# Hybrid decoder trunk: high weight parts cast two jobs ahead into a third buffer, decays in the big pool

## Chip, cores and metric

The kernel runs on one core of a Trainium2 chip. The metric is the device time of one execution in microseconds. PE is TensorE, DVE is VectorE, ACT is ScalarE, POOL is GpSimd, and SP is the engine that issues every DMA here.

## What is computed

One decoder layer on 512 tokens of width 1024, all in float32 (cut to its flow):

```python
u = rmsnorm(x, ln1_g)
q, k, v, pool_in, z, xbc, dt_raw, gate_pre = split(u @ w_in)
y_a = dilated_attention_mixer(q, k, v, rel_bias) @ w_a      # 3 groups of 6 heads
y_b = pool_mixer(pool_in, pool_w, pool_scale) @ w_b         # causal means of 2, 4, 8, 16 steps
y_c = ssd_mixer(z, xbc, dt_raw, ...) @ w_c                  # 4 chunks of 128, 2 groups of 8 heads
gates = sigmoid(gate_pre + b_gate)
x = x + (gates[0] * y_a + gates[1] * y_b + gates[2] * y_c) @ w_o
h = causal_dwconv(rmsnorm(x, ln2_g) @ w_up)                 # 2 x 2816 columns
x = x + (silu(h[:2816]) * h[2816:]) @ w_down
return rmsnorm(x, final_g)
```

In the SSD part the decay between two tokens of a chunk is `exp(a_cs[l] - a_cs[s])` for each head.

## The kernel before

**Three products for one.** A float32 operand is written as a high part in a rounded 32-bit format (`F32R`) and a low part, which is the difference. Each matrix product is the sum of three: high by high, high by low, low by high (`mm3`, `chunk_a`). So each weight tile goes through four steps: `fetch` has SP load it from DRAM as `raw` (1 MB for a full tile), ACT casts it into the high part `wh`, DVE subtracts to get the low part `wl`, and PE uses both. `raw`, `wh` and `wl` have two buffers each.

**Jobs.** The whole kernel is a list of weight tiles with a body each, 94 jobs, run one after the other by the loop at the end of `trunk`. In the order of that list they are: pool input 0 to 3, gates of the pool branch 4 to 7, pool products 8, w_b 9 to 12, the three attention groups 13 to 27 (two jobs for v and three for q and k in each), xbc 28 to 33, gates of the attention branch 34 to 37, gates of the SSD branch and z mixed 38 to 45, w_a 46 and 47, w_c 48 to 51, w_o 52 to 59, w_up 60 to 81, w_down 82 to 93. Most have 48 matmuls of 512 columns. The w_a jobs have 36 with a smaller tile, the eight w_o jobs 24, because they are done for two blocks of 128 tokens at a time, and the last of each half of w_down 24.

**The order.** PE, ACT, DVE and POOL run in the order in which the program is written (`ORDERED`); SP's order is found by the scheduler. Between the matmuls of a job, `step()` lets waiting side work advance by one piece: attention items, SSD items, norms. So each engine's queue is a mixture of evacuations of PSUM, side work, and the preparation of weights, and an instruction that waits holds up all that is written behind it on its engine.

**Preparation.** At the start of job n its `prepare` casts the tile of job n+1 and takes its low part, then fetches n+2 and n+3 where that has not been done (a fetch waits until the buffer is free, that is until the low part of the tile two before it is taken). Up to job 33 cast and low part are made in two halves of the columns, the second half at the job's first `step()` through the list `second`. From job 34 on they are made in one piece. A few jobs are `late`: they call `prepare` from their own body (the last w_o job and the first two w_up jobs), so that norm work comes ahead of it.

**Side work at the places that the prediction speaks of.** `y_norm(gi)` norms the SSD output of one group while the w_a jobs run: PE sums squares into `pss`, DVE and ACT make the root, DVE builds the diagonal `dg`, PE spreads it over the rows (`prb`, L875), DVE scales (L878), ACT casts the result to `yth`, DVE takes `ytl` (L885); w_c needs these. `wo_jobs` adds the product to x (L930), ACT sums its squares (`junk`, L294), DVE norms it to `u` (L335), and PE transposes `u` (`uT`, L307) for w_up. `ssd_item` loads the decays of one chunk and group: two tiles `al` of 256 KB each, from their own pool `alp` of six buffers (L754 to L759), which DVE (L785), ACT (L786) and DVE (L790) turn into the masks that PE reads for `py` (L800). All other side work takes its tiles from one pool, `big`, of 52 buffers of 128 x 512 values.

Of the kernel before, what the change touches and what calls it, by code (L numbers as in the profile page):

```python
# [10 lines left out]
F32 = mybir.dt.float32  # L11
F32R = mybir.dt.float32r
# [4 lines left out]
P = 128  # L17
S = 512
# [63 lines left out]
def trunk(ctx: ExitStack, tc, out, x, rel_bias, ln1_g, w_in, b_gate, w_a, pool_w, pool_scale, w_b,  # L82
# [9 lines left out]
    cpool = ctx.enter_context(tc.tile_pool(name="const", bufs=1))  # L92
    rows = ctx.enter_context(tc.tile_pool(name="rows", bufs=1))
    wraw = ctx.enter_context(tc.tile_pool(name="wraw", bufs=2))
    wspl = ctx.enter_context(tc.tile_pool(name="wspl", bufs=2))
    upool = ctx.enter_context(tc.tile_pool(name="upool", bufs=1))
    big = ctx.enter_context(tc.tile_pool(name="big", bufs=NBIG))
    alp = ctx.enter_context(tc.tile_pool(name="alp", bufs=6))
    ypool = ctx.enter_context(tc.tile_pool(name="ypool", bufs=2))
    tiny = ctx.enter_context(tc.tile_pool(name="tiny", bufs=8))  # L100
    psum = ctx.enter_context(tc.tile_pool(name="psum", bufs=4, space=bass.MemoryType.PSUM))
# [3 lines left out]

    def T(name, dt=F32, shape=(P, S)):
        return big.tile(list(shape), dt, name=name, tag="t")

    def A(name):
        return alp.tile([P, S], F32, name=name, tag="al")  # L110

    def MM(name):
        return psum.tile([P, S], F32, name=name, tag="mm")
# [51 lines left out]
                sp.dma_start(raw[:, :, at:at + n], src[:, :, i * n:(i + 1) * n])  # L165
                at += n

    def split(job, cuts=1, later=False, eng=None, halves=False):
        k, c = job.k, job.c
        h = wspl.tile([P, k, c], F32R, name="wh", tag="wh")  # L170
        l = wspl.tile([P, k, c], F32R, name="wl", tag="wl")
        w = c // cuts
        job.split = h, l
        def high(i):
            o = slice(i * w, (i + 1) * w)
            act.copy(h[:, :, o], job.raw[:, :, o])  # L176

        def low(i):
            o = slice(i * w, (i + 1) * w)
            (eng or dve).tensor_tensor(l[:, :, o], job.raw[:, :, o], h[:, :, o].bitcast(F32),  # L180
                                       OP.subtract)

        def lows():
            for i in range(cuts):
                low(i)
                yield

        if halves:
            high(0)
            low(0)  # L190
            second.append(lambda: (high(1), low(1)))
            return
        for i in range(cuts):
            high(i)
        if later:
            return lows()
        for _ in lows():
            pass

    def wsrc(w, k0, k1, c0, c1):  # L200
# [550 lines left out]
    def ssd_item(c, gi):  # L751
        cs = slice(c * P, (c + 1) * P)
        dtv, acs, dec, tot, ad, ed = (cst[n] for n in ("dtv", "acs", "dec", "tot", "ad", "ed"))
        als = []  # L754
        for q in range(2):
            al = A("al")
            h0 = 8 * gi + 4 * q
            sp.dma_start(al.rearrange("p (h l) -> p h l", h=4), ad[h0:h0 + 4, cs].partition_broadcast(P))
            als.append(al)  # L759
        if c:  # L760
            ea = T("ea")
            for i in range(2):
                h0 = 8 * gi + i
                sp.dma_start(ea[DH * i:DH * i + DH].rearrange("p (j l) -> p j l", j=4),
                             ed[h0:h0 + 8 - i:2, cs].partition_broadcast(DH))
        ps = SM("pxs")
        for j in range(4):
            pe.transpose(ps[:, j * P:(j + 1) * P], XS[4 * gi + j][:, cs], eye)
        xc = T("xc")
        dve.tensor_tensor(h3(xc), h3(ps), hb(dtv, c, 8 * gi), OP.mult)  # L770

        y = Y[gi][:, :, cs]
        pcb = SM("pcb")
        pe.matmul(pcb[:, :P], XS[8 + gi][:, cs], XS[10 + gi][:, cs], start=True, stop=True)
        cbt = T("cbt", F32, (P, P))
        dve.tensor_tensor(cbt, pcb[:, :P], tri, OP.mult)
        if c < 3:
            xd = T("xd")
            pool.tensor_tensor(h3(xd), h3(xc), hb(dec, c, 8 * gi), OP.mult)
        yield  # L780
        for q in range(2):
            a3 = als[q].rearrange("p (h l) -> p h l", h=4)
            for j in range(4):
                i = c * SH + 8 * gi + 4 * q + j
                dve.tensor_scalar(a3[:, j, :], a3[:, j, :], acs[:, i:i + 1], 0.0, OP.subtract, OP.min)  # L785
            act.activation(als[q], als[q], AF.Exp)  # L786
        yield
        for q in range(2):
            a3 = als[q].rearrange("p (h l) -> p h l", h=4)
            dve.tensor_tensor(a3, a3, cbt.unsqueeze(1).to_broadcast([P, 4, P]), OP.mult)  # L790
        yield
        if c and c < 3:
            nw = T("st")
            pool.tensor_tensor(h3(nw), h3(prev[gi]), hb(tot, c, 8 * gi), OP.mult)
        yield
        py = SM("py")
        for j in range(4):
            for i in range(2):
                o, lo = (2 * j + i) * DH, (2 * j + i) % 4 * P
                pe.matmul(py[DH * i:DH * i + DH, j * P:(j + 1) * P], xc[:, o:o + DH],  # L800
                          als[j // 2][:, lo:lo + P], start=True, stop=True)
        by_j = lambda t: t.rearrange("p (j l) -> p j l", j=4)
        if c:
            po = SM("pyo")
            for j in range(4):
                pe.matmul(po[:, j * P:(j + 1) * P], prev[gi][:, j * P:(j + 1) * P], XS[10 + gi][:, cs],  # L806
                          start=True, stop=True)
            dve.tensor_tensor(ea, po, ea, OP.mult)
            dve.tensor_tensor(ea, ea, py, OP.add)
        for j in range(4):  # L810
            m = 4 * gi + j
            dve.scalar_tensor_tensor(y[:, j, :], y[:, j, :], cst["dgc"][:, m:m + 1],
                                     by_j(ea if c else py)[:, j, :], OP.mult, OP.add)
        done.add((c, gi))
        if c < 3:
            pst = SM("pst")
            pe.matmul(pst, btok[gi][:, cs], xd, start=True, stop=True)  # L817
            if c == 0:
                nw = T("st")
                act.copy(nw, pst)  # L820
            else:
                dve.tensor_tensor(nw, nw, pst, OP.add)
            prev[gi] = nw
# [359 lines left out]
    def begin(n, lo, hi, between=lambda early: None):  # L1183
        wh, wl = weights[n].split
        order = [(wh, uh, 0)]
        for k in range(1, KD):
            order += [(wh, uh, k), (wh, ul, k - 1)]
        order.append((wh, ul, KD - 1))
        for part in (order, [(wl, uh, k) for k in range(KD)]):
            for a, b, k in part:  # L1190
                for j in range(2):
                    pe.matmul(first[2 * n + j][:, lo:hi], a[:, k, j * P:(j + 1) * P], b[:, k, lo:hi],
                              start=a is wh and b is uh and k == 0, stop=a is wl and k == KD - 1)
            between(part is order)
        if hi == S:
            for j in range(2):
                pool_evac(2 * n + j, first[2 * n + j])
                step()
# [17 lines left out]
                turn_scale(0, k)  # L1216
    pe.transpose(first[2][:, :KD], g8[:KD, :P], eye[:KD, :KD])
    dve.tensor_copy(g1, first[2][:, :KD])
    split(weights[0], 2, eng=pool)
    for k in range(KD):  # L1220
        turn_scale(1, k % 2 * 4 + k // 2)
    for k in range(KD):
        turned(k, 0, bank(k))
    low = split(weights[1], 2, later=True)


    ss = row_squares(2, small("ss", [P, 4]), 2)
    next(low)
    r = rstd_of(ss, 2, D)
    for tb in (2, 3):  # L1230
        for h in range(2):
# [2 lines left out]
                dve.tensor_scalar(t, t, r[:, tb - 2:tb - 1], None, OP.mult)  # L1234
            else:
                act.mul(t, t, r[:, tb - 2:tb - 1])
    next(low)
    begin(0, 0, 256)

    def turns(early):  # L1240
# [12 lines left out]
    fetch(weights[2])  # L1253
    fetch(weights[3])
    begin(0, 256, S)
    split(weights[2])
    begin(1, 256, S)


    n = 0  # L1260
    for job in jobs:
        if not isinstance(job, Job):
            job.fn()
            continue
        flush()
        if n >= 2:
            def prepare(n=n, later=False):
                low = None
                if n + 1 < len(weights) and weights[n + 1].split is None:
                    if later or weights[n].short or not HALVES[0] <= n < HALVES[1]:  # L1270
                        low = split(weights[n + 1], later=True)
                    else:
                        split(weights[n + 1], 2, halves=True)

                def rest():
                    for _ in low or ():
                        pass
                    for m in (n + 2, n + 3):
                        if m < len(weights) and weights[m].raw is None:
                            fetch(weights[m])  # L1280
                if later:
                    return rest
                rest()

            if job.late:
                job.prepare = prepare
            else:
                prepare()
            job.body(job.split)
        n += 1  # L1290
# [2 lines left out]

# [1 line left out]
ORDERED = {EngineType.PE, EngineType.Activation, EngineType.DVE, EngineType.Pool}  # L1295
NBIG = 52
HALVES = 0, 34
MIX = "gggZZ0zzg1aa"
SSD_ORDER = ((0, 0, 1), (1, 0, 1), (0, 1, 1), (2, 0, 1), (1, 1, 1), (3, 0, 1), (2, 1, 1), (3, 1, 1))
WARM = 12  # L1300
# [29 lines left out]
```

## Time and profile before

| | us |
|---|---|
| median of 3 runs | 1065.72 |
| lowest to highest | 1065.25 to 1068.02 |
| profiled execution, its own time | 1067.88 |
| its span, first to last instruction | 1065.7 |
| mean granted clock of TensorE | 0.994 |
| DMA queue, share of its 16 engines | 35.4% |
| read from HBM | 110.87 MB |

The page gives busy time by engine, the busy share in slices of the span, the DMA queues, the chain of work that ended last, and the costliest groups of instructions. A timeline row is: start, length, engine, line, operation, what is written from what is read, shapes, count, and in brackets how long the engine had been idle and what ended that. A row of the waits is: who waited for whom, us in total, times, longest. A row of the windows is: the stretch, its length, busy time (and instructions) of PE, PEld (weight loads), DVE, ACT and POOL, then the granted clock, the DMA share and GB/s.

### The profile page before, as it was taken

What the parts mean: (1) busy time and instruction counts of PE and PEld (TensorE: products, weight loads), DVE (VectorE), ACT (ScalarE), POOL (GpSimd) and SP (SyncE); (2) the same over time, 40 slices, a digit from 0 to 9 for tenths busy, and PEclk for the clock granted to TensorE, in tenths of its full rate; (3) what the DMA queues carried; (4) which work ended last, traced back from release to release, by engine and by line L of the source; (5) the groups of instructions that cost most, each with busy time, mean ns of one, the idle gap of its engine ahead of it and who ended that gap; (6) DMA issues with size and microseconds to landing.
All of it is one profiled execution on the core that took longest, in us unless ns stands there. A gap on an engine that the chain in (4) does not pass through costs nothing.

```text
span 1065.7 us, 12968 instructions
## 1 busy us (share of the span) xinstructions
PE 1047.1 (98%) x5268; PEld 874.1 (82%) x5268; DVE 584.9 (55%) x809; ACT 427.8 (40%) x640; POOL 133.3 (13%) x118
## 2 busy tenths in 40 slices
PE   8999999999999999999999799999999999999997
PEld 8878889888988888877888588898888888888885
DVE  5562433245544668586687856757655565542315
ACT  5342412232435356555544324544444344421312
POOL 1680000000000000621012300001111111110100
PEclk9999999999999999999999899999999999999999
DMA  7235324341542222654322135543232323232312
GB/s 235 77 107 158 109 73 108 98 110 60 143 110 77 81 79 79 178 164 126 90 77 98 54 114 198 163 138 117 83 117 79 117 82 115 83 119 61 117 60 79
DMA packets 116426, 115.50 MB, mean 108 GB/s; under 512 B 5235, under 2 KB 101302, under 8 KB 116367
## 3 DMA queue, kind: packets, MB, share of 16 engines
q1 hardware_dynamic: 116367, 114.68, 35.4%
q8 instruction: 41, 0.67, 0.3%
q14 instruction: 18, 0.15, 0.0%
HBM read 110.87 MB, written 2.22 MB: 106 GB/s over the span
## 4 chain that ended last, share of the span: by engine, by line
PE 93%; DVE 2%; issue 2%; ACT 1%; DMA 1%; POOL 0%; SPq 0%; DVEq 0%; ACTq 0%; POOLq 0%
PE pa L209 33%; PE pu L209 22%; PE pb L209 20%; PE pqk L209 9%; PE ps L500 1%; PE po L539 1%; PE pt L527 1%; PE ppw L209 1%; DVE ytl L885 1%; PE py L800 1%; PE pu L1027 1%; DMA raw<-in_w_in_dram 1%; PE pyo L806 1%; PE pst L817 1%; ACT wh L176 0%
## 5 line engine op out<-in xcount | busy, mean ns | idle before, releaser
L180 DVE TENSOR_TENSOR wl<-raw,wh 128x2048 fp32r<-128x2048 f32 (+4 forms) x126 | 220.8, 1755 | 252.5 <-ACT wh L176 252.4
L176 ACT CAST wh<-raw 128x1024 fp32r<-128x1024 f32 (+4 forms) x128 | 179.4, 1408 | 123.3 <-PE pb L209 76.6
L209 PE MATMUL pa<-uh,wh 128*128 128x512 f32 x384 | 98.3, 398 | 0.3 <-ACT wh L176 0.3
L209 PE MATMUL pa<-ul,wh 128*128 128x512 f32 x384 | 94.9, 389 | 0.0
L994 DVE SCALAR_TENSOR_TENSOR hc<-pu,fcol,hc 128x510 f32<-128x510 f32 x88 | 65.8, 748 | 53.1 <-ACT hc L991 51.5
L209 PE MATMUL pa<-uh,wl 128*128 128x512 f32 x384 | 94.8, 389 | 0.0
L209 PEld LDWEIGHTS pa<-ul,wh 128*128 128x128 f32 x384 | 72.1, 188 | 15.2
L209 PEld LDWEIGHTS pa<-uh,wl 128*128 128x128 f32 x384 | 72.1, 188 | 15.0
L209 PE MATMUL pu<-ul,wh 128*128 128x512 f32 (+1 forms) x352 | 83.5, 379 | 0.0
L209 PE MATMUL pu<-uh,wl 128*128 128x512 f32 (+1 forms) x352 | 83.5, 379 | 0.0
L209 PE MATMUL pu<-uh,wh 128*128 128x512 f32 (+1 forms) x352 | 83.5, 379 | 0.0
L209 PEld LDWEIGHTS pa<-uh,wh 128*128 128x128 f32 x384 | 70.2, 188 | 15.5 <-issue 0.9
L209 PEld LDWEIGHTS pu<-uh,wl 128*128 128x128 f32 x352 | 64.2, 188 | 12.5
L209 PEld LDWEIGHTS pu<-ul,wh 128*128 128x128 f32 x352 | 64.2, 188 | 12.5
L209 PEld LDWEIGHTS pu<-uh,wh 128*128 128x128 f32 x352 | 64.1, 188 | 12.4
L991 ACT ACTIVATE hc<-pu,fcol,fcol 128x512 f32<-128x512 f32 x40 | 31.1, 780 | 81.0 <-PE pu L209 81.0
L999 POOL TENSOR_TENSOR hc<-hc 128x512 f32<-128x512 f32 x22 | 31.5, 1430 | 223.7 <-DVE hc L994 223.6
L521 ACT ACTIVATE sb<-sb,nm 128x128 f32<-128x128 f32 (+1 forms) x72 | 30.1, 419 | 64.4 <-DVE nm L518 49.0
L587 POOL TENSOR_TENSOR nmT<-nmT,dtmp 6x512 f32<-6x512 f32 x3 | 5.6, 1896 | 351.8 <-DVE dtmp L583 351.8
L209 PE MATMUL pb<-wh,fh 128*128 128x512 f32 x176 | 47.7, 389 | 0.0
L209 PE MATMUL pb<-wl,fh 128*128 128x512 f32 x176 | 47.7, 389 | 0.0
L209 PE MATMUL pb<-wh,fl 128*128 128x512 f32 x176 | 47.7, 389 | 0.0
(272 smaller groups left out, 1611.2 us busy)
## 6 DMA issues: line engine op xcount, KB each, us to landing
raw<-in_w_in_dram SPq DMA_DIRECT2D x25, 1024.0 KB
raw<-in_ffn_w_up_dram SPq DMA_DIRECT2D x22, 1024.0 KB
raw<-in_w_in_dram SPq DMA_DIRECT2D x20, 512.0 KB
raw<-in_ffn_w_down_dram SPq DMA_DIRECT2D x10, 1024.0 KB
raw<-in_w_o_dram SPq DMA_DIRECT2D x8, 1024.0 KB
raw<-in_w_in_dram SPq DMA_DIRECT2D x6, 768.0 KB
raw<-in_w_b_dram SPq DMA_DIRECT2D x4, 1024.0 KB
al<-ad SPq DMA_DIRECT2D x16, 256.0 KB
```

The costliest lines, as they stand in the source:

```text
L176: act.copy(h[:, :, o], job.raw[:, :, o])
L180: (eng or dve).tensor_tensor(l[:, :, o], job.raw[:, :, o], h[:, :, o].bitcast(F32), OP.subtract)
L209: pe.matmul(ps, l, r, start=first and n == 0, stop=last and n == total - 1)
L500: pe.matmul(pss[i][:, o:o + w * P], q[r, n * P:(n + 1) * P], k[r, kb * P:(kb + w) * P], start=True, stop=True)
L521: act.activation(sb[:, off:off + w * P], sb[:, off:off + w * P], AF.Exp, bias=nm[:, n, h:h + 1], accum_out=ls[:, n, h:h + 1])
L527: pe.transpose(pt[:, o:o + P], sb[:, o:o + P], eye)
L539: pe.matmul(po[DH * hh:DH * hh + DH, n * P:(n + 1) * P], V[g, kb + i][:, (2 * c + hh) * DH:(2 * c + hh + 1) * DH], probs[2 * c + hh, nb][: ...
L800: pe.matmul(py[DH * i:DH * i + DH, j * P:(j + 1) * P], xc[:, o:o + DH], als[j // 2][:, lo:lo + P], start=True, stop=True)
L806: pe.matmul(po[:, j * P:(j + 1) * P], prev[gi][:, j * P:(j + 1) * P], XS[10 + gi][:, cs], start=True, stop=True)
L991: act.activation(t, ps, AF.Identity, bias=ff["c1"][:, ff["b"] + m:ff["b"] + m + 1], scale=fw(2, m))
L994: dve.scalar_tensor_tensor(t[:, sh:], ps[:, :S - sh], fw(k, m), t[:, sh:], OP.mult, OP.add)
L999: pool.tensor_tensor(a, a, t, OP.mult)
```

## The change

The high parts get a pool of their own, `whp`, with three buffers; the low parts keep two (`wlp`). `split` becomes two functions: `cast` makes the high part on ACT, `lows` and `low` the low part. At the start of job n the new `prepare` takes the low part of n+1, whose cast is already made, in one piece, then casts n+2 in two halves of the columns (the second half at the first `step()`; in `late` jobs both at once), then fetches n+3. For this the tile of job 3 is cast and that of job 4 fetched ahead of the loop. `HALVES` goes. The pool `alp` goes too: the decays `al` are now tiles of `big`, which has 54 buffers instead of 52.

```diff
-    wspl = ctx.enter_context(tc.tile_pool(name="wspl", bufs=2))
+    whp = ctx.enter_context(tc.tile_pool(name="whp", bufs=3))
+    wlp = ctx.enter_context(tc.tile_pool(name="wlp", bufs=2))
...
-    alp = ctx.enter_context(tc.tile_pool(name="alp", bufs=6))
...
-    def split(job, cuts=1, later=False, eng=None, halves=False):
...
+    def cast(job, cuts=1, spread=False):
+
+        w = job.c // cuts
+        job.high = whp.tile([P, job.k, job.c], F32R, name="wh", tag="wh")
+
         def high(i):
             o = slice(i * w, (i + 1) * w)
-            act.copy(h[:, :, o], job.raw[:, :, o])
...
+            act.copy(job.high[:, :, o], job.raw[:, :, o])
+
+        for i in range(cuts):
+            if spread and i:
+                second.append(lambda i=i: high(i))
+            else:
+                high(i)
+
+    def lows(job, cuts=1, eng=None):
+
+        w, h = job.c // cuts, job.high
+        l = wlp.tile([P, job.k, job.c], F32R, name="wl", tag="wl")
+        job.split = h, l
+        for i in range(cuts):
             o = slice(i * w, (i + 1) * w)
             (eng or dve).tensor_tensor(l[:, :, o], job.raw[:, :, o], h[:, :, o].bitcast(F32),
                                        OP.subtract)
...
+            yield
+
+    def low(job, cuts=1, eng=None):
+        for _ in lows(job, cuts, eng):
             pass
...
         for q in range(2):
-            al = A("al")
+            al = T("al")
...
     begin(0, 256, S)
-    split(weights[2])
+    cast(weights[2])
+    low(weights[2])
     begin(1, 256, S)
+    cast(weights[3])
+    fetch(weights[4])
...
             def prepare(n=n, later=False):
-                low = None
-                if n + 1 < len(weights) and weights[n + 1].split is None:
-                    if later or weights[n].short or not HALVES[0] <= n < HALVES[1]:
-                        low = split(weights[n + 1], later=True)
-                    else:
-                        split(weights[n + 1], 2, halves=True)
-
                 def rest():
-                    for _ in low or ():
-                        pass
-                    for m in (n + 2, n + 3):
-                        if m < len(weights) and weights[m].raw is None:
-                            fetch(weights[m])
+                    if n + 1 < len(weights):
+                        low(weights[n + 1])
+                    if n + 2 < len(weights):
+                        cast(weights[n + 2], 2, spread=not later)
+                    if n + 3 < len(weights):
+                        fetch(weights[n + 3])
                 if later:
                     return rest
                 rest()
...
-NBIG = 52
-HALVES = 0, 34
+NBIG = 54
```

More of the change, by code (lines that the diff above doesn't have):

```diff
@@ L107, in T @@
         return big.tile(list(shape), dt, name=name, tag="t")
-    def A(name):
-        return alp.tile([P, S], F32, name=name, tag="al")
     def MM(name):
@@ L166, in fetch @@
                 at += n
-    def split(job, cuts=1, later=False, eng=None, halves=False):
[L169 to L173, printed above, removed]
+    def cast(job, cuts=1, spread=False):
+        w = job.c // cuts
+        job.high = whp.tile([P, job.k, job.c], F32R, name="wh", tag="wh")
         def high(i):
             o = slice(i * w, (i + 1) * w)
-            act.copy(h[:, :, o], job.raw[:, :, o])
-        def low(i):
+            act.copy(job.high[:, :, o], job.raw[:, :, o])
[9 more added lines that the diff above has]
+        for i in range(cuts):
             o = slice(i * w, (i + 1) * w)
@@ L181, in low @@
                                        OP.subtract)
[L183 to L197, printed above, removed]
+            yield
+    def low(job, cuts=1, eng=None):
+        for _ in lows(job, cuts, eng):
             pass
@@ L1218, in trunk @@
     dve.tensor_copy(g1, first[2][:, :KD])
-    split(weights[0], 2, eng=pool)
+    cast(weights[0], 2)
+    low(weights[0], 2, pool)
     for k in range(KD):
@@ L1223, in trunk @@
         turned(k, 0, bank(k))
-    low = split(weights[1], 2, later=True)
+    cast(weights[1], 2)
+    parts = lows(weights[1], 2)
     ss = row_squares(2, small("ss", [P, 4]), 2)
-    next(low)
+    next(parts)
     r = rstd_of(ss, 2, D)
@@ L1236, in trunk @@
                 act.mul(t, t, r[:, tb - 2:tb - 1])
-    next(low)
+    next(parts)
     begin(0, 0, 256)
```

## The prediction

> **What bounds the kernel now.** I read the page first, then the windows of 20 us, the waits of each engine, and the chain in order of time.
>
> ```profile
> span 1065.7 us, 12968 instructions
> PE 1047.1 (98%) x5268; PEld 874.1 (82%) x5268; DVE 584.9 (55%) x809; ACT 427.8 (40%) x640; POOL 133.3 (13%) x118
> ```
> ```profile
> 580.00:600.00 20.00, 16.09 (x63) 12.26 (x62) 17.99 (x24) 6.42 (x8) 8.46 (x6) 0.83 0.27 88
> 600.00:620.00 20.00, 17.00 (x68) 13.38 (x67) 11.99 (x15) 4.36 (x6) 2.94 (x2) 0.91 0.22 70
> ...
> sum 1060.00, PE 1047.08 PEld 874.12 DVE 583.17 ACT 427.46 POOL 133.26; mean PE 19.76 PEld 16.49 DVE 11.00 ACT 8.07 POOL 2.51
> ```
> The page's first column gives TensorE 1047.1 of 1065.7 us, so 18.6 us are idle. In the windows (length, then busy time of PE, PEld, DVE, ACT, POOL, then the granted clock) 6.9 of them, 3.91 + 3.00, lie between 580 and 620, and only there does the clock fall under 1. The rest lies in the first 40 us and after the last matmul, and the change leaves both as they are. So whatever VectorE and ScalarE are spared elsewhere is hidden behind matmuls, and a gain has to come from this one place.
>
> ```profile
> DVE wl L180 <- ACT wh L176: 252.4, 92, 10.5
> ...
> PE prb L875 <- DVE dg L871: 3.9, 1, 3.9
> PE pa L209 <- ACT yth L880: 3.0, 1, 3.0
> ```
> The waits say what the two gaps wait for. They also hold a tempting number: VectorE waits 252.4 us for high casts, and the change takes that whole wait away. Nearly all of its 92 pieces lie beside busy matmuls and cost nothing today. The chain finds the one that does:
>
> ```profile
> 579.19 1.48 ACT wh L176
> ...
> 580.70 1.76 DVE wl L180
> 582.45 1.19 DVE sg L901 x2
> 583.65 3.00 DVE ytl L885 x2
> 586.65 1.32 DVE xs L878 x2
> 587.97 1.20 DVE sg L901 x2
> 589.16 2.99 DVE ytl L885 x2
> ...
> 593.51 0.70 DVE dg L871
> ...
> 594.26 2.08 PE prb L875 x2
> 596.34 5.57 PE pa L209 x18
> ...
> 601.93 0.69 DVE sg L901
> 602.61 2.27 DVE ytl L885 x2
> 604.88 0.67 DVE xs L878
> ...
> 605.58 0.63 ACT yth L880
> ```
> Here the SSD output is normed while the two w_a jobs run. Job 47's high cast on ScalarE holds up its low part on VectorE, and behind that stand the evacuations and norm steps up to dg, for which TensorE waits.
>
> **The first gap.** The timeline gives the idle time in front of that low part, and the end of the matmuls before the gap:
>
> ```profile
> 580.40 0.84 PE L209 MATMUL pa<-ah,wl 128*128 128x512 f32 x3
> 580.70 1.76 DVE L180 TENSOR_TENSOR wl<-raw,wh 128x1536 fp32r<-128x1536 f32 x1 [2.12 <-ACT wh L176]
> ...
> 589.51 0.84 PE L209 MATMUL pa<-ah,wl 128*128 128x512 f32 x3
> ```
> After the change job 47 is cast during job 45, so the low part starts 2.12 us earlier, at 578.58. Not all of it arrives: the second sg must wait for its matmuls, which end at 580.40 + 0.84 = 581.24, where VectorE would be ready at about 580.93. That leaves 2.12 - 0.35 = 1.75 us. From there to dg VectorE runs without a break, so dg ends at 592.45 instead of 594.2. TensorE stops at 589.51 + 0.84 = 590.35 as before, and the gap shrinks from 3.9 to about 2.15 us. What is late next is the same row of VectorE work, now without a hole. ScalarE gets two half casts of job 48 in this stretch; they stand beside VectorE's row, which covers them.
>
> **The clock behind the gap.** Windows cut where the granted clock changed:
>
> ```profile
> 589.09:592.50 3.41, 1.26 (x6) 0.72 (x4) 3.14 (x5) 1.07 (x3) 2.52 (x2) 1.00 0.00 0
> 592.50:595.91 3.41, 1.65 (x3) 0.84 (x3) 3.16 (x7) 1.75 (x1) 0.00 (x0) 0.50 0.00 0
> ...
> 602.74:606.15 3.41, 0.51 (x3) 0.09 (x1) 3.41 (x4) 0.57 (x1) 1.60 (x1) 1.00 0.00 0
> 606.15:609.56 3.41, 3.31 (x7) 2.44 (x8) 2.28 (x4) 2.47 (x3) 0.00 (x0) 0.50 0.00 0
> ```
> A window of 3.41 us in which TensorE worked 1.26 or 0.51 us is followed by half clock; one with 1.65 us leaves it at half, one with 3.31 us ends it. Half clock ran from 594.26 to 599.33 and cost half of that, 2.5 us. With the same cuts, work would resume at 592.5, fill the window to 595.91 and be at full clock there: cost 1.7, gain 0.85. The second gap stays 3.0 us long, because sg, ytl, xs and yth (601.93 to 606.2) follow TensorE's own end; but it ends at about 603.8, so half clock lasts 2.35 instead of 3.4 us: gain 0.45 to 0.5. Together 1.75 + 0.85 + 0.45 is about 3.0 us. The cuts needn't fall at the same places in another execution. Bounds: nothing (the clock eats the shift) to 5.5 (first rival).
>
> The page "TensorE: Matmul & The Clock Gate" of the Trainium skill (Why this matters for your kernels) asks only that no gap be over about 3 us, the gate closing after one idle window. The 602.74 row speaks against it: a gap of 3.0 us, with 0.51 us of work in its window, closed it. By the rule the shorter gap would be free, which is the first rival.
>
> **What the change adds: transfers come one job nearer.** Until now job n cast job n+1, and its raw tile had been fetched long before. Now job n casts half of n+2 at its start, and that tile's fetch left only in job n-1, after a low part. Casts and fetches stand in the queues of ScalarE and SP ahead of everything that job n issues. Prices:
>
> ```profile
> L180 DVE TENSOR_TENSOR wl<-raw,wh 128x2048 fp32r<-128x2048 f32 x56 | 135.7, 2423 | 137.3 <-ACT wh L176 137.2
> L176 ACT CAST wh<-raw 128x1024 fp32r<-128x1024 f32 x58 | 60.1, 1045 | 44.9 <-PE pb L209 26.2 <-PE pa L209 15.4 <-PE pqk L209 2.1
> ```
> ```profile
> 684.27 7.47 SPq L165 DMA_DIRECT2D raw<-in_ffn_w_up_dram  x2
> ...
> 689.56 1.92 ACT L176 CAST wh<-raw 128x2048 fp32r<-128x2048 f32 x1 [0.54 <-DMA raw<-in_ffn_w_up_dram]
> ```
> A fetch of 1 MB issued at 684.27 let a waiting cast start at 689.56: 5.2 us. Low 2.3, fetch 5.2, half cast 1.05: 8.6 us. A job of 48 matmuls takes 10.9 us (next fence), so most jobs cover it. The eight w_o jobs (52 to 59) have 24 matmuls, 5.5 us, and do not:
>
> ```profile
> 664.58 2.29 DVE L180 TENSOR_TENSOR wl<-raw,wh 128x2048 fp32r<-128x2048 f32 x1 [1.65 <-ACT wh L176]
> ...
> 670.75 0.63 ACT L294 ACTIVATE junk<-x 128x512 f32<-128x512 f32 x1 [2.95 <-DVE x L930]
> ...
> 676.19 1.00 DVE L335 TENSOR_SCALAR u<-xg,r,rt 128x512 f32<-128x512 f32 x2
> ...
> 677.43 1.91 PE L307 MATMUL uT<-eye,u 128*128 128x128 f32 x16
> ...
> 679.34 10.93 PE pb L209 x48
> ```
> The low part of job 55 ends at 664.58 + 2.29 = 666.9 today; behind a second half cast that now stands after the squares of job 53 I put it at 667.3. So job 57's raw lands at 672.5, its first half cast ends at 673.5, and only then come the squares that ran at 670.75: 2.8 us late. They lead through two norm chains to the u of 676.19, which would end at about 680 instead of 677.19. TensorE needs its first half when eight of the sixteen transposes are done, at 677.43 + 0.96 = 678.4, and gets it half a microsecond before the end, at 679.5 to 679.6: 1.2 us idle. Job 57's second half cast waits behind those norms on ScalarE, its low part behind u on VectorE (to 682.4); the next fetch lands at 687.5; and by job 59 the casts and low parts come some 0.7 us after TensorE wants them. That makes 1.9 us. Bounds: none, if the raw is there 1.5 us sooner; 6 us, if each fetch of this stage takes a microsecond more, for the ring of low, fetch and cast carries a delay from job to job.
>
> **Edits costed at nothing.** 46 late casts become two halves, 0.2 us of ScalarE each (2 x 1.045 against 1.92); low parts before job 34 become one piece. ScalarE is at 40%, VectorE at 55%, with full TensorE above them; without that cover, 9 us. The decays:
>
> ```profile
> 436.77 1.64 DVE L785 TENSOR_SCALAR al<-al,acs 128x128 f32<-128x128 f32 x8
> 446.23 2.74 DVE L180 TENSOR_TENSOR wl<-raw,wh 128x2048 fp32r<-128x2048 f32 x1 [7.81 <-ACT wh L176]
> ```
> Their own pool let the first six be loaded long ahead; in the big pool they come in program order, between the wb loads. L785 waits for them and with it VectorE's queue, low parts and evacuations. But VectorE idles 7.81 us right behind the first L785, so that much lateness is free. SP's waits for a free decay buffer go, and no matmul waited for those. I take 0, bounds -0.5 and +2.
>
> **The sum.** -3.0 + 1.9 is about -1.0 us. The profiled execution took 1067.88 us, its span 1065.7 and 2.2 around it; it would be 1066.9. It stands 2.2 above the median of the runs, 1065.72, so for the median I say 1064.7. About 0.3%, 3.2 us, is what a measurement of this kernel can tell from no change.
>
> **Rivals.** (1) The clock stays full over both gaps. Then the work behind dg (594.26 to 601.91, less the 2.5 us of half clock: 5.1) ends at 597.6, VectorE's row (low 2.3, two sg 1.2, two xs 1.3, two sg 1.2 from 592.5 on) at 598.6 is the bound, the second gap ends 3.3 to 3.8 us earlier, and the 1.65 us after it go too: -5.2. With 0.4 to 1.9 lost at w_o the net is -3.3 to -4.8, 1061.7 in the middle. For it: the gap falls to 2.15 us, and cut in two by a window's edge it leaves more than 2 us of work in each. Against it: with the cuts of this trace the window still has 1.26 us. Chance 0.24.
> (2) The raw ring is the bound at w_o: each fetch of jobs 55 to 61 lands over 6 us after its issue, squares and casts wait in turn, and 6 us are lost against 2 to 3 won: 1069.3. It decides from one microsecond above the 5.2 of today. For it: those fetches now run beside the eight x1 loads and one another. Against it: the single row above. Chance 0.34.
> (3) The forecast, between them: 0.42. That the cast isn't moved cannot be: the code has only the new order.
>
> **Numbers.** The forecast's own range is 1062.6 to 1068.5; with the rivals 1061.2 to 1070.5. Faster 0.24, within 0.3% 0.42, slower 0.34.
>
> **What would show it.** Right: no wait of wl for wh; the wait of prb for dg about 2.2 us; ScalarE waiting for raw in jobs 53, 55 and 57; TensorE waiting about a microsecond for u before uT. Wrong: prb still 3.9 us late; TensorE waiting anywhere between 440 and 560, which would put the decays or their queue on the path; or w_o jobs without a wait for raw.

## The result and the profile after

The changed kernel takes 1075.62 us in the median of four runs (1073.98 to 1077.22), beside 1065.49 for the kernel before on the same chip. The ratio is 1.0090, with an interval of 1.0068 to 1.0112: 0.9% slower. The prediction said 1064.7, with a range that ended at 1070.5.

The profiled execution took 1073.98 us, the shortest of the four. The page, the first two lines:

```profile
span 1072.1 us, 13001 instructions
...
PE 1047.6 (98%) x5268; PEld 873.8 (82%) x5268; DVE 576.8 (54%) x777; ACT 432.0 (40%) x698; POOL 130.0 (12%) x118
```

The span is 6.4 us longer, and TensorE worked as long as before (1047.1), so the time went into gaps. The windows of the changed kernel (columns as in the prediction) say where:

```profile
440.00:460.00 20.00, 19.10 (x98) 15.30 (x97) 8.90 (x13) 7.67 (x9) 9.62 (x8) 1.00 0.61 161
460.00:480.00 20.00, 15.89 (x86) 12.26 (x85) 11.86 (x27) 11.28 (x14) 4.33 (x4) 1.00 0.57 154
480.00:500.00 20.00, 19.34 (x92) 15.48 (x93) 12.12 (x29) 10.04 (x12) 3.09 (x3) 0.91 0.62 166
...
680.00:700.00 20.00, 17.41 (x84) 13.84 (x83) 13.70 (x21) 10.94 (x18) 2.55 (x2) 1.00 0.33 107
```

Before, TensorE had no gap from 440 to 500 nor from 680 to 700. Now it has 5.7 us of them in the first stretch, with a drop of the clock behind, and 2.6 in the second. The waits give the names:

```profile
PE pcb L769 <- DVE ea L803: 4.8, 1, 4.8
PE pa L204 <- ACT yth L875: 3.6, 1, 3.6
PE prb L870 <- DVE dg L866: 1.8, 1, 1.8
PE uT L302 <- DVE u L330: 1.2, 1, 1.2
PE pb L204 <- ACT wh L172: 1.1, 1, 1.1
```

```profile
DVE al L780 <- DMA al<-ad: 31.9, 8, 13.9
...
ACT wh L172 <- DMA raw<-in_w_o_dram: 18.0, 3, 6.5
...
DVE wl L187 <- ACT wh L172: 17.4, 6, 10.3
```

VectorE's wait for high casts fell from 252.4 to 17.4 us, as the change intends. In its place VectorE waits 31.9 us for the decays `al`, once for 13.9, and TensorE 4.8 us for the evacuation `ea`. To put a number on each place I read the end of the last matmul of every job in both timelines. The difference moves at these jobs only:

```
change of a job's end against the kernel before (us)
the opening, before job 0          -1.15
job 34 (gates, attention branch)   +0.65
jobs 37 and 38 (SSD starts)        +7.55
jobs 46 to 48 (norm gaps)          -3.66
jobs 57 and 59 (w_o)               +3.15
all others together                -0.09
```

The opening differs from execution to execution; without it the change costs 7.6 us in this trace. The first gap fell from 3.9 to 1.8 us as forecast, and the w_o loss came where it was forecast. What turned the sum is the line of jobs 37 and 38: 1.2 us of it in job 37, 6.4 in job 38.

**How the decays stop TensorE.** SP's rows of the kernel before, the loads around the start of the SSD part:

```profile
284.49 4.44 SPq L758 DMA_DIRECT2D al<-ad  x6
```

```profile
434.77 8.94 SPq L594 DMA_DIRECT2D wb<-wd  x12
...
444.39 3.86 SPq L594 DMA_DIRECT2D wb<-wd  x6
```

The first six decay tiles were loaded at 284, some 150 us ahead of their use. From 434 to 448 SP issues 18 loads of `wb` (the weights of the attention groups, 128 KB each), with raw fetches ahead of and between them. The changed kernel:

```profile
431.96 5.82 SPq L589 DMA_DIRECT2D wb<-wd  x8
...
438.52 2.90 SPq L589 DMA_DIRECT2D wb<-wd  x4
441.54 1.06 SPq L753 DMA_DIRECT2D al<-ad  x2
...
456.69 0.38 SPq L162 DMA_DIRECT2D raw<-in_w_in_dram  x1
...
458.44 1.11 SPq L753 DMA_DIRECT2D al<-ad  x2
```

The `al` of the first item (the SSD work of one chunk and group) now stand behind twelve `wb` and leave at 441.54. What VectorE and TensorE make of it (brackets: idle before, and what ended it):

```profile
449.77 4.69 DVE L780 TENSOR_SCALAR al<-al,acs 128x128 f32<-128x128 f32 x8 [13.90 <-DMA al<-ad]
...
454.38 2.28 DVE L187 TENSOR_TENSOR wl<-raw,wh 128x2048 fp32r<-128x2048 f32 x1
...
456.72 2.11 PE L204 MATMUL pa<-uh,wl 128*128 128x512 f32 x8 [0.90 <-DVE wl L187]
...
464.48 1.87 DVE L780 TENSOR_SCALAR al<-al,acs 128x128 f32<-128x128 f32 x4 [5.81 <-DMA al<-ad]
...
480.67 0.80 PE L769 MATMUL pcb<-xcv 128*128 128x128 f32 x2 [4.78 <-DVE ea L803]
```

VectorE reaches the step on `al` at 435.9, 5.7 us before they leave, and the first is there 8.2 us after its issue. So it waits 13.9 us, and then works on them until 454.5. Behind it in its queue stands the low part of job 37: TensorE waits 0.90 us for that, until 456.72. And it goes round: the raw fetch at 456.69 waits for this low part, the second item's `al` (458.44) stand behind that fetch on SP, VectorE waits for them 5.8 us at 464.48, the next low part comes late, and the next raw fetch and the third item with it. At 480.67 TensorE has waited 4.8 us with `pcb` for `ea`, whose step (it reads PSUM) stands behind that low part on VectorE. The half clock that follows runs from 480.33 to 483.74. So the round costs far more than the first wait.

### The profile page after: what moved, and what is told of

Read it like the earlier page. It is cut to its first block, busy times and chain, and to the rows that moved or that the text cites. A ratio compares the mean times of both kernels' runs of the same rounds, so it can differ in the third digit from the quotient of the medians.

```text
span 1072.1 us, 13001 instructions
## 1 busy us (share of the span) xinstructions
PE 1047.6 (98%) x5268; PEld 873.8 (82%) x5268; DVE 576.8 (54%) x777; ACT 432.0 (40%) x698; POOL 130.0 (12%) x118
## 4 chain that ended last, share of the span: by engine, by line
PE 84%; DVE 5%; DMA 5%; ACT 3%; issue 2%; SPq 1%; POOL 0%; DVEq 0%; ACTq 0%; POOLq 0%
PE pa L204 28%; PE pu L204 21%; PE pb L204 17%; PE pqk L204 9%; DMA raw<-in_w_o_dram 2%; DMA wb<-wd 1%; DMA al<-ad 1%; DVE wl L187 1%; PE ps L495 1%; PE pu L1022 1%; PE pt L522 1%; PE ppw L204 1%; PE po L534 1%; ACT wh L172 1%; DVE ytl L880 1%
## 5 line engine op out<-in xcount | busy, mean ns | idle before, releaser
L187 DVE TENSOR_TENSOR wl<-raw,wh 128x2048 fp32r<-128x2048 f32 (+3 forms) x94 | 216.5, 2304 | 106.1 <-PE pb L204 68.1
L172 ACT CAST wh<-raw 128x1024 fp32r<-128x1024 f32 (+2 forms) x186 | 187.9, 1026 | 151.6 <-PE pb L204 57.9
```

Source lines behind the costliest of these rows:

```text
L172: act.copy(job.high[:, :, o], job.raw[:, :, o])
```

## Experiments

Each was timed in five rounds beside the kernel before, whose median in these three sessions was 1067.38, 1066.92 and 1066.93. So ratios are compared, or medians within one session. Theory A: the decays' loads in program order cost the 7.5 us. Theory B: the new order of casts, low parts and fetches is late by itself, and the decays only stand beside it.

**1. The change with the decays in their own pool**

```diff
+    alp = ctx.enter_context(tc.tile_pool(name="alp", bufs=6))
...
-            al = T("al")
+            al = alp.tile([P, S], F32, name="al", tag="al")
...
-NBIG = 54
+NBIG = 48
```

> The changed kernel with the decays back in a pool of their own of six buffers, and 48 buffers in the big pool (the same memory). Theory A, decays: in the big pool they are loaded in program order, behind the wb loads and behind raw fetches, VectorE waits for them at the head of its queue, and jobs 37 and 38 lose 7.5 us by it. Then the loss of jobs 37 and 38 goes and what is left is the shorter norm gap (-3.6), job 34 (+0.65) and the w_o jobs (+3.2): 1066 us, 1064.5 to 1067.5. Theory B, order of preparation: the low parts and fetches of the two-ahead order are themselves late, the decays only stand beside them: 1072 us or more, with TensorE still waiting for wl or ea between 440 and 490.

Measured 1066.67 us, ratio 0.9992 (0.9983 to 1.0001): no different from the kernel before, 0.98% better than the changed kernel by the ratios. SP's row, and the windows:

```profile
280.99 4.16 SPq L754 DMA_DIRECT2D al<-ad  x6
```

```profile
440.00:460.00 20.00, 20.00 (x105) 16.07 (x104) 16.80 (x19) 14.48 (x17) 15.02 (x10) 1.00 0.69 187
460.00:480.00 20.00, 20.00 (x106) 16.21 (x106) 13.79 (x29) 7.13 (x9) 3.30 (x3) 1.00 0.59 164
480.00:500.00 20.00, 20.00 (x111) 15.88 (x112) 11.60 (x23) 12.25 (x15) 2.05 (x2) 1.00 0.45 134
```

The loads are back at 281, and TensorE is full from 440 to 500. What is left of the change is a gain and a loss that cancel.

**2. The kernel before with only the decays moved**

```diff
-    alp = ctx.enter_context(tc.tile_pool(name="alp", bufs=6))
...
-            al = A("al")
+            al = T("al")
...
-NBIG = 52
+NBIG = 58
```

> The kernel before, with only the decays moved into the big pool (58 buffers, the same memory), casts as before. Theory A: the first decays are loaded in program order, between the wb loads, and TensorE loses about 7 us between 440 and 490: 1073 us, 1070 to 1075. Theory B: without the two-ahead order the low parts have their slack of 7.8 us and the lateness stays hidden, as the prediction had it: 1065.5 us, within 2.

Measured 1074.66, ratio 1.0066 (1.0053 to 1.0078). Theory A; the casts need not be touched to lose 7 us. The place is the same, but the victim is another:

```profile
451.52 0.88 DVE L781 TENSOR_SCALAR al<-al,acs 128x128 f32<-128x128 f32 x4 [14.18 <-DMA al<-ad]
...
455.01 1.88 ACT L172 CAST wh<-raw 128x2048 fp32r<-128x2048 f32 x1
...
456.95 2.57 PE L205 MATMUL pa<-uh,wh 128*128 128x512 f32 x8 [3.68 <-ACT wh L172]
```

With the old order it is ScalarE's queue: the cast of job 37 stands behind the exponent of the late `al` and ends at 456.89, and TensorE waits 3.68 us for it. So whatever is prepared behind the late load is what TensorE misses.

**3. Decays in the big pool, but loaded early** (`decays` takes the two `al` tiles of an item and issues their loads)

```diff
     def ssd_start():
+        for c, gi, _ in SSD_ORDER[:3]:
+            early[c, gi] = decays(c, gi)
...
     def ssd_item(c, gi):
-        als = []
...
+        als = early.pop((c, gi), None) or decays(c, gi)
```

> The changed kernel, decays in the big pool of 54, but the tiles of the first three items (six tiles) are taken and loaded where the SSD part starts (job 34), ahead of the wb loads. Theory A in its form that the order of the loads and not the pool is what costs: no DVE wait for al over 3 us before 470, jobs 37 and 38 as before, 1066.5 us, 1065 to 1069. If the shared buffers themselves were the cost (buffers that come free late), it stays near 1075.

Measured 1065.96, ratio 0.9989 (0.9979 to 0.9999).

```profile
415.68 6.42 SPq L753 DMA_DIRECT2D al<-ad  x6
```

The six loads leave at 415.68, ahead of the `wb`. So the pool is not the cost: its buffers were there, and only the place of the loads in SP's order counts.

**4. One item early instead of three**

```diff
-        for c, gi, _ in SSD_ORDER[:3]:
+        for c, gi, _ in SSD_ORDER[:1]:
```

> The changed kernel, decays in the big pool of 54, only the first SSD item's two tiles loaded where the SSD part starts (three items' six tiles gave 1066). Theory A says the first item's 14 us late start is what pushes all the rest, and the second item loses because its loads stand behind a raw fetch that waits for a low part that waits for the first item. Then one item is nearly enough: 1067 us, 1065 to 1069, and the second item's al costs VectorE under 5 us of wait. If each item in the stretch is late by itself, since every load comes in program order, one item early gives back only the first part: 1070 to 1073.

Measured 1066.38, ratio 0.9998 (0.9989 to 1.0007): one item is enough. The second half of the expectation missed. The second item's `al` cost VectorE 7.26 us, not under 5:

```profile
454.54 2.11 DVE L787 TENSOR_SCALAR al<-al,acs 128x128 f32<-128x128 f32 x4 [7.26 <-DMA al<-ad]
```

```profile
440.00:460.00 20.00, 20.00 (x106) 16.09 (x104) 11.91 (x15) 11.95 (x14) 13.46 (x10) 1.00 0.76 205
460.00:480.00 20.00, 20.00 (x106) 16.21 (x106) 13.56 (x33) 9.68 (x12) 3.09 (x3) 1.00 0.67 171
```

TensorE is busy throughout all the same. So 7 us of waiting at the second item is covered, while the 14 at the first, with the round that they start, are not.

**5. Late casts in the w_o jobs** (on top of experiment 1)

```diff
-            if spread and i:
+            if spread and (i or end):
                 second.append(lambda i=i: high(i))
...
-                        cast(weights[n + 2], 2, spread=not later)
+                        cast(weights[n + 2], 2, spread=not later, end=weights[n].short)
```

> As the run with the decays in their own pool, and in the eight short w_o jobs both halves of the cast of n+2 are made at the end of job n instead of the first at its start. The prediction's mechanism at w_o: the first half cast stands in ScalarE's queue and waits there for the raw tile, the norms behind it. If so the 3.2 us of jobs 57 and 59 go, TensorE is idle under 0.5 us between 660 and 700, and the time is 3 us under that of the first run: 1063. If instead the fetches themselves are late (each over 6 us behind the low part), the waits move to the low parts and it is within 1 us of the first run.

Measured 1063.86 beside 1066.67 in the same session: 2.8 us less. Ratio 0.9967 (0.9955 to 0.9980). ScalarE's two rows in the changed kernel, and the windows of this run:

```profile
675.94 1.05 ACT L172 CAST wh<-raw 128x1024 fp32r<-128x1024 f32 x1 [5.59 <-DMA raw<-in_w_o_dram]
...
692.23 1.05 ACT L172 CAST wh<-raw 128x1024 fp32r<-128x1024 f32 x1 [5.88 <-DMA raw<-in_w_o_dram]
```

```profile
660.00:680.00 20.00, 20.00 (x98) 16.78 (x97) 16.36 (x25) 11.60 (x20) 0.91 (x1) 1.00 0.40 147
680.00:700.00 20.00, 19.96 (x114) 17.14 (x113) 13.61 (x26) 10.04 (x18) 2.59 (x2) 1.00 0.45 152
```

In the changed kernel the first half casts wait 5.6 and 5.9 us for the raw tile, the squares behind them. Moved behind the squares, the casts no longer wait for a w_o tile, and TensorE is idle 0.04 us between 660 and 700.

**6. The cast of job 47 late again** (on top of 5)

```diff
+                    if n == 46:
+                        cast(weights[47])
...
-                    if n + 2 < len(weights):
+                    if n + 2 < len(weights) and n != 45:
```

> The version with own decay buffers and late casts at w_o (1063.9), but the high part of job 47 alone is cast at the start of job 46 again, in one piece ahead of its low part. The prediction's first step: this one cast carries the whole gain of the change. Then TensorE's wait for dg goes from 1.8 back to 3.9 us, half clock follows it, and the time is 3 to 5 us longer: 1067.5. If the gain came from the other early casts and low parts, the change is under 1 us.

Measured 1066.86, ratio 0.9999 (0.9990 to 1.0008), against 0.9967 of the version it starts from.

```profile
PE prb L871 <- DVE dg L867: 3.9, 1, 3.9
```

The wait for dg is back at 3.9 us, and 0.32% of the time has come back with it, about 3.4 us. Of the 92 waits for a high cast, this one was worth something: nearly all the others are still gone in this run, and it is no faster than the kernel before.

**7. Filling the second gap** (on top of 5)

```diff
+                        for k in range(6):
+                            pe.matmul(ps, wh[:, k, :P], xh(k), start=k == 0, stop=False)
+                        spare = MM("spare")
+                        for q in range(12):
+                            pe.matmul(spare, uhk(0)[:, :P], uhk(1), start=True, stop=True)
...
```

> The same version (1063.9) with 12 matmuls of 128x512 into an unused PSUM tile between the sixth and seventh matmul of the first w_c tile, where TensorE waits 3.7 us for yth. They add 2.7 us of work inside the wait. Theory of the prediction: the half clock after the second gap, 1.7 to 3.4 us, comes from the empty window alone. Then the granted clock stays 1.00 between 600 and 620 and the time is about 2 us shorter: 1062. If the throttle does not follow the empty window, or the matmuls delay the rest, 1064 or more.

Measured 1063.33, ratio 0.9969 (0.9958 to 0.9981): not to be told from the 0.9967 without it. In the profiled execution the clock does what the theory says, and job 48 takes 2.2 us less than in the profile of experiment 5:

```profile
600.00:620.00 20.00, 18.93 (x83) 15.11 (x82) 14.02 (x16) 5.33 (x7) 1.50 (x1) 1.00 0.18 54
```

The medians do not show it (1063.33 and 1063.86), so the 2 us that were expected did not come. The profiled execution of experiment 5, at 1065.22, was the slowest of its five, 1.4 us over their median, which may be part of it; the rest stays open.

**8. The norm's order in the second gap** (on top of 5). For the second SSD group the two `xs` come ahead of the four `ytl`, and the first w_c job takes its products with the weight's low part before those with `ytl` (`lower` makes the `ytl` of m). The two parts of the edit were not tried apart:

```diff
-            if j % 2:
-                yield
-                for q in (m - 1, m):
-                    dve.tensor_sub(YT[q][1], Y[gi][:, q % 4, :], YT[q][0].bitcast(F32))
+            if j == 1:
+                yield
+            if j % 2 and not gi:
+                if j == 3:
+                    yield
+                lower(m - 1)
+                lower(m)
+        if gi:
+            for q in range(4):
+                lower(4 + q)
...
-        for a, b in ((wh, xh), (wh, xl), (wl, xh)):
+        for a, b in ((wh, xh), (wl, xh), (wh, xl)) if turn else ((wh, xh), (wh, xl), (wl, xh)):
```

> The same version (1063.9); for the second SSD group the two xs steps that end in yth come ahead of the low parts ytl on VectorE, and the first w_c job multiplies by the weight's low part before it needs the ytl. Now 3.0 us of ytl stand ahead of the xs for which TensorE waits 3.7 us. If VectorE's order is what makes the second gap, it falls to under 1.5 us, the clock stays full behind it, and the time is 3 to 5 us shorter: 1060. If the low parts are simply waited for instead, the wait moves to ytl and it is within 1 us of 1063.9.

Measured 1059.43, ratio 0.9932 (0.9919 to 0.9946). The wait for yth fell from 3.7 to 1.0 us in two pieces, and the clock stayed at 1.00:

```profile
PE pa L205 <- ACT yth L879: 1.0, 2, 0.8
```

```profile
600.00:620.00 20.00, 19.84 (x87) 16.19 (x88) 13.23 (x15) 6.17 (x8) 0.34 (x1) 1.00 0.31 106
```

**9. The same edit on the kernel before.** The diff is that of experiment 8, with nothing else changed.

> The kernel before with the one edit of the last run (second group's xs and yth ahead of the ytl, the first w_c job's low part of the weights first), none of the change. If that edit is worth the same without the change, its 4.4 us come off the kernel before: 1062.5. If the first gap of 3.9 us keeps the clock at half into w_c, or the gain needs the early cast of job 47 and its low part, less than 2 us come off.

Measured 1063.20, ratio 0.9962 (0.9949 to 0.9976): 3.7 us off. The edit is worth about as much with the change as without it; together with the early cast of job 47 and the repairs of experiments 1 and 5 it gives the 1059.4.

**10. Low parts of jobs 47 and 48 on GpSimd** (on top of 8)

```diff
-                        low(weights[n + 1])
+                        low(weights[n + 1], 1, pool if n in (46, 47) else dve)
```

> The version with the new norm order (1059.4), with the low parts of jobs 47 and 48 made on GpSimd. VectorE is busy 19 of 20 us from 580 to 600 and loses 4 us of work by this. If VectorE's work is all that counts, the first gap (1.7 us) goes and the time is 1057.5. The rival: in these traces VectorE's tensor steps on SBUF operands take about twice as long while GpSimd is at work (ytl 0.68 us alone, 1.13 beside it). Then the two low parts, 4 us or more each on GpSimd, slow the rest of the row, and the time is 1059.4 or longer.

Measured 1065.09, ratio 0.9982 (0.9972 to 0.9991): some 5 us slower than the version it starts from. The rival held, by more than it said. GpSimd's row and then VectorE's:

```profile
589.82 4.96 POOL L188 TENSOR_TENSOR wl<-raw,wh 128x2048 fp32r<-128x2048 f32 x1
```

```profile
590.97 3.84 DVE L281 TENSOR_TENSOR rt<-r 128x4 f32<-128x4 f32 x1
594.84 0.16 DVE L282 TENSOR_TENSOR rt<-rt,v 128x4 f32<-128x4 f32 x1
```

The step `rt` on 128x4 values, whose like right behind it takes 0.16 us, took 3.84 us, and it ended at 594.81, where GpSimd's low part ends (589.82 + 4.96 = 594.78). Behind it dg came late, and TensorE waited 5.2 us for it.

**11. No sums on GpSimd beside the norm** (on top of 8). VectorE makes them later:

```diff
-            (dve if last else pool).tensor_tensor(MG[m], MG[m], s, OP.add)
+            if not last:
+                MA[m] = s
+                return
+            dve.tensor_tensor(MG[m], MG[m], MA[m], OP.add)
+            dve.tensor_tensor(MG[m], MG[m], s, OP.add)
```

> The same version (1059.4), where the eight sums of the gated branches that GpSimd makes during the w_a jobs are made by VectorE later, in the w_c jobs, where it has room. VectorE's own work between 575 and 600 is unchanged. If GpSimd slows VectorE, the two ytl that take 3.09 us beside these sums take about 1.4, dg is ready 1.7 us earlier, the first gap falls under 0.4 us: 1057.7. If the slow ytl have another reason, nothing changes there: 1059.4.

Measured 1057.19, ratio 0.9909 (0.9894 to 0.9924). VectorE's rows of the `ytl`, of experiment 8 and then of this one, and TensorE's wait for dg:

```profile
587.30 3.09 DVE L873 TENSOR_TENSOR ytl<-xs,yth 128x512 fp32r<-128x512 f32 x2
```

```profile
585.42 1.29 DVE L873 TENSOR_TENSOR ytl<-xs,yth 128x512 fp32r<-128x512 f32 x2
```

```profile
PE prb L871 <- DVE dg L867: 0.2, 1, 0.2
```

The two `ytl` take 1.29 us instead of 3.09, and the first gap falls from 1.7 to 0.2 us. This version is the shortest of all: 0.9% under the kernel before, 1.8% under the changed one.

## Where the prediction was right and where it failed

**The failed step** is the one headed "Edits costed at nothing", the decays: taken at 0, bounds -0.5 and +2; measured +7.55 in the trace of the changed kernel, and 0.66% of the time alone (experiment 2). The argument was that VectorE idles 7.81 us behind the first L785, so that much lateness is free. The runs don't speak against that: the wait of 13.9 us itself left TensorE idle for 0.90 us (that of 14.18 in experiment 2 for 3.68), and the wait of 7.26 at the second item in experiment 4 for none. What the step lacked is two things. The lateness was never worked out, though the kernel before had rows for its larger causes: six loads at 284.49, and 13 us of SP's time for 18 `wb` and a raw fetch from 434.77 to 448.25, in whose midst the new place of the loads is. And it took the lateness as paid once, at the first item. The next raw fetch waits for VectorE's late low part and the next `al` stand behind that fetch, so the delay came back, and job 38 lost 6.4 us by it, against 1.2 in job 37. The text said "between the wb loads" and stopped there, and a bound of 2 us had no row behind it. The sign that it named, TensorE waiting between 440 and 560, is what came.

**The first gap**: right. 2.15 us were forecast and 1.8 came, and experiment 6 shows that the one cast of job 47 carries it.

**The clock** came out better at the first gap and worse at the second. Windows of the changed kernel, cut where its granted clock changed:

```profile
596.38:599.79 3.41, 1.66 (x7) 0.88 (x6) 2.96 (x9) 2.09 (x3) 0.00 (x1) 1.00 0.00 0
...
606.62:610.03 3.41, 0.63 (x2) 0.32 (x3) 3.33 (x5) 1.41 (x3) 0.70 (x1) 1.00 0.00 0
610.03:613.45 3.42, 3.42 (x9) 2.68 (x10) 2.74 (x2) 0.76 (x1) 0.00 (x0) 0.50 0.00 0
```

The window with 1.66 us of work left the clock at 1.00; the prediction had read the row with 1.65 us as one that leaves it at half. Both are true: in these two cases such a window changed nothing, and the clock stayed what it was. The one with 0.63 us was followed by half clock. The other traces fit. Cut in the same way, from 20 us to the last matmul, every window at full clock with 1.49 us of work or less (experiment 2, 455.02 to 458.44, has the 1.49) was followed by half clock, and none with 1.66 or more was. At half clock, windows with up to 2.76 us (experiment 4, 600.81 to 604.22) stayed there, and those with 3.08 or more ended it. So that part of the first rival came true which concerns the first gap. It agrees with the rule of the Trainium skill that the prediction weighed (page "TensorE: Matmul & The Clock Gate", Why this matters for your kernels), which asks that no gap be over about 3 us: this gap was 1.8 us. The second gap, forecast at 3.0, was 3.6 us. Two `ytl` stand in it, 2.35 us long in the timeline of the kernel before, beside one of GpSimd's sums (602.69), and 2.95 now, beside four (601.85 to 607.32):

```profile
601.85 5.47 POOL L900 TENSOR_TENSOR sg<-sg 128x512 f32<-128x512 f32 x4 [5.47 <-DVE sg L896]
...
604.93 2.95 DVE L880 TENSOR_TENSOR ytl<-xs,yth 128x512 fp32r<-128x512 f32 x2
```

The net of jobs 46 to 48 is -3.66, where the sum had -3.0. That the two lie so close is partly luck: up to the end of job 47 4.6 us are won, where the sum had 2.6 (1.75 and 0.85), and job 48 loses 0.9 of them, where the sum had 0.45 won.

**The w_o jobs**: mechanism right, size 3.15 instead of 1.9, within its bounds. ScalarE's three waits for raw came (18.0 us in all), TensorE waited 1.23 us for u, as worked out (1.2), and at job 59 1.1 for the high part and 0.2 for the low, instead of 0.7; the other 0.6 us are not in waits. The chain has the three fetches on which ScalarE waited:

```profile
658.88 5.31 DMA raw<-in_w_o_dram
...
670.81 5.03 DMA raw<-in_w_o_dram
...
685.56 6.59 DMA raw<-in_w_o_dram
```

The sum had put each at 5.2 us. The last took 1.4 more, and job 59 lost 1.0 more than forecast. So the condition of the second rival, over 6 us, held for the last fetch, not for the other two, and its price of 6 us did not come; experiment 5 shows that the place of the casts is what makes the fetches matter at all.

**Not foreseen and not tested**: 0.65 us at job 34. And the trace explains 7.6 us, while the medians stand 10.1 apart: the profiled execution was the shortest of its kernel, and the kernel before was between 1064.2 and 1069.5 over all sessions, so 1 us (against the 1067 of the later sessions) to 2.5 us of this are not assigned.

## What to carry to other kernels

A tile that moves from its own pool into a shared one keeps its memory but loses its head start: here its load left where the program stands, behind what the DMA-issuing engine had queued there, until experiment 3 took the tiles and loaded them early. So work out the new landing time from the issue rows, with the time in flight, and compare that with the slack of the first instruction that waits, before the edit is costed at nothing. And one long wait of an in-order engine for a load can feed itself, when the next fetches stand behind what that engine still has to do.

## What the runs showed of the hardware

VectorE was slowed by GpSimd to more than twice its time, and once held outright: `ytl` took 0.65 us each alone and 1.5 beside GpSimd's sums (experiment 11), and a step of 0.16 us was held for 3.84 until a GpSimd instruction ended (experiment 10). The page "SBUF — State Buffer" of the Trainium skill (SBUF: two separate sides) describes it as a lock: a VectorE step with two inputs from SBUF and a GpSimd step that reads SBUF exclude each other for the length of a whole instruction. The row of 590.97 agrees, to 0.03 us: both inputs of that step are `r`, in SBUF. The two steps ahead of it, with one tensor input each, ran beside the same GpSimd instruction at 590.34 and 590.76, in 0.15 and 0.18 us. In this stretch, where VectorE's row sets the first gap, work handed to GpSimd was no relief: taking eight sums off GpSimd gave 2 us, and giving it two low parts cost some 5.
